# A two-layer decoder trunk: the index projection ordered by hand, PSUM banks swapped, three gate projections moved

## The chip, the cores and the metric

The kernel runs on one core of a Trainium2 chip. A core has five engines that work side by side and wait for one another through semaphores: TensorE (PE in the profile; its weight loads are PEld), VectorE (DVE), ScalarE (ACT), GpSimd (POOL) and SyncE (SP), which here only issues transfers. The metric is the device time of one execution, in microseconds. The time before is 760.7 us, the median of three runs (760.47 to 761.76).

## The reference, cut to what matters

`x` is 512 positions by 1024 channels, float32. Layer 0 is a gated mixer (a matrix memory and causal pooling); layer 1 is sparse attention. Layer 1 in short:

```python
xn = rmsnorm(x, g_norm)
q, ckv, qi, ki, wi, z = _split(xn @ w_in, ODD_SPLITS)   # 1024, 256, 4*64, 64, 4, 1024 columns
q = rmsnorm(q.reshape(hd), g_q)                         # 16 heads x 64
ckv = rmsnorm(ckv, g_kv)
k = rmsnorm((ckv @ w_uk).reshape(hd), g_k)
v = (ckv @ w_uv).reshape(hd)
# for each block of 128 queries
score = einsum('bqh,bqhs->bqs', wib, relu(einsum('bqhd,bsd->bqhs', qib, ki)))   # causal
_, idx = lax.top_k(score, 128)
logits = einsum('bqhd,bqkhd->bqhk', qb, k[idx]) * C_HEAD_DIM ** -0.5 + bias
out = einsum('bqhk,bqkhd->bqhd', softmax(logits), v[idx])
return x + (out * jax.nn.silu(z)) @ w_out
```

So three things come out of one input projection that matter below: the index part (`qi`, `ki`, `wi`, 324 columns), which decides which keys each query may see; the gates `z` (1024 columns, 64 for each of 16 heads); and the query and latent parts that feed the attention.

## The kernel before, in words

Activations lie with channels on the 128 partitions (`xT`, `xn_h`, `xn_l`: 8 blocks of 128 channels by 512 tokens). Every large product is made of three float32r matmuls: high part by high part, and the two mixed ones. So each weight tile is loaded by SP (`raw`), its high part cast on ACT (`wh`, L147), and its low part subtracted on DVE or POOL (`wl`, L148). A capital letter in an order list puts that subtraction on DVE, a small one on POOL. Three such tiles are in flight.

Layer 0 ends with its output projection. `next_x` (L605) adds a channel block to `xT` on DVE (L606), stores it, scales it into `xn_h` and `xn_l` (L241 on ACT, L242 on DVE), squares it (L250 on ACT) and adds the square to `ssum` on POOL (L251). `norm_factors` (L253) then sums `ssum` over the partitions on PE (L257), adds the epsilon on DVE, takes the power on POOL (L260, `r4`) and spreads the factors over the partitions with one more product (L265), copied on ACT to `r_bc`. `xn` of layer 1 is not yet normalised: the factors are applied where a projection's result leaves PSUM.

Layer 1 begins with the index projection: four token tiles `t` of 128, each of 8 channel blocks times 3 matmuls of 324 columns (L180 to L182). `ev_idx` (L637) scales the result on ACT into `qk_tok` (L640, L641), transposes it on PE (L645) and splits it into `qi` and `ki`. Then an order list, `ORDER` (L54), runs the steps: `i` scores of a query block, `C` the latent projection, `s` a quarter of a block's selection (rounds of MAX8, L725, and MATCH_REPLACE8, L726, on DVE), `q`, `k`, `v` projections of a group of four heads, `z` the gates of a group (two blocks of 24 matmuls of 512 columns, scaled on DVE, L803, SiLU on ACT, L804), `a` the attention of a group and a query block (exponential on ACT, L834, normalising on ACT, L836, transposes on PE, L844, product with v, L853 to L855, gate on DVE, L859), and `y` the split of finished results. The output projection of layer 1 follows.

What a list gives is a priority, not the last word. `TileContext(schedule_with_timeline_sim=True)` plans the order on each engine from estimated costs: where an instruction isn't ready in the plan, a later one goes ahead. Each engine then executes its queue strictly in that order.

PSUM has eight banks of 128x512 float32. `psum_pools` closes the pools and lays new ones from the first bank on. Layer 0 has `mm=4` in the first four banks and `bg=4` in the others. Layer 1 has `mm=3, qk=1, tr=2, po=1` (a `qk` tile takes two banks); `bg()` then means `tr`. A new tile waits for those who still use the bank.

Of the kernel before, what the change touches and what calls it, by code (L numbers as in the profile page):

```python
# [12 lines left out]
ALU = mybir.AluOpType  # L13
# [4 lines left out]
NT = 4  # L18
NK = 8
# [31 lines left out]
ORDER_A = ("z0 E0 k0 Q0 O0 W0 R0 Q1 k1 W1 R1 E1 v2 Y0 O1 Q2 k2 W2 k3 V3 z1 R2 q3 W3 R3 Y1")  # L51


ORDER = ("i1 i2 C i3 s10 q0 z0 k0 z2 v0 s11 v1 Z1 K1 Q1 s12 s13 s20 s21 s22 a00 Z3 s30 s23 s31 K2 s32 a01 a02 a10 s33 a12 a03 q2 V2 k3 a20 a23 a21 a13 a11 Q3 V3 a22 a33 a31 a32 y32 y31 y0 a30 y33 y30 y1 y2")  # L54


@with_exitstack
def trunk(ctx: ExitStack, tc: tile.TileContext, a: dict, out: bass.AP):
    nc = tc.nc
    V, A, G, T = nc.vector, nc.scalar, nc.gpsimd, nc.tensor  # L60
# [5 lines left out]
    ps = {}  # L66
    ps_pools = ExitStack()

    def psum_pools(**banks):
        ps_pools.close()  # L70
        ps.clear()
        for n, b in banks.items():
            ps[n] = ps_pools.enter_context(tc.tile_pool(name="ps_" + n, bufs=b, space=PSUM))

    ctx.callback(ps_pools.close)
    psum_pools(mm=4, bg=4)

    def bank(n):
        return ps[n].tile([128, 512], F32, name=n)

    def mm():
        return bank("mm")
    dr = ctx.enter_context(tc.tile_pool(name="dr", bufs=1, space=bass.MemoryType.DRAM))

    def bg():
        return bank("bg" if "bg" in ps else "tr")
# [3 lines left out]
    ident = cst[:, O_IDENT:O_IDENT + 128]  # L90
# [20 lines left out]
    def sub_f32r(dst, src, h):  # L111
        V.tensor_tensor(dst, src, h.bitcast(F32), op=ALU.subtract)  # L112

    def split(h, l, src):
        A.copy(h, src)  # L115
        sub_f32r(l, src, h)
# [9 lines left out]
    def run(order, **step):  # L126
        for w in order.split():
            low_engine[0] = V if w[0].isupper() else G
            step[w[0].lower()](*map(int, w[1:]))
# [4 lines left out]
    def wtile(shape, loads, queue=nc.sync):  # L134
        n = math.prod(shape)
        raw = wp.tile([128, 1024], F32, name="raw", bufs=3)
        wh = wp.tile([128, 1024], F32R, name="wh")
        wl = wp.tile([128, 1024], F32R, name="wl")

        def view(t):  # L140
            t = t[:, :n]
            if len(shape) == 2:
                t = t.rearrange("p (x y) -> p x y", x=shape[0])
            return t
        for sl, src in loads:
            queue.dma_start(view(raw)[:, sl[0], sl[1]], src)
        A.copy(wh[:, :n], raw[:, :n])  # L147
        low_engine[0].tensor_tensor(wl[:, :n], raw[:, :n], wh[:, :n].bitcast(F32), op=ALU.subtract)  # L148
        return view(wh), view(wl)
# [3 lines left out]
    def wrows(w, r0, nk, c0, n):  # L153
        return w[r0:r0 + 128 * nk, c0:c0 + n].rearrange("(k p) c -> p k c", p=128)

    def wcols(cols, kk, queue=nc.sync):
        loads, off = [], 0
        for w, c0, m in cols:
            loads.append(((ALL, slice(off, off + m)), wrows(w, 128 * kk[0], len(kk), c0, m)))
            off += m  # L160
        return wtile([len(kk), off], loads, queue)

    def dense_tok(act, ks, cols, evac, groups=(range(NT),), share=False):

        n = sum(x[2] for x in cols)
        step = min(1024 // n, len(ks))
        ws = {}

        def part(t, k0, ps):
            kk = ks[k0:k0 + step]
            if k0 not in ws:
                ws[k0] = wcols(cols, kk)
            wh, wl = ws[k0]
            for j, k in enumerate(kk):
                ah, al = act(k)
                ts = slice(128 * t, 128 * t + 128)
                first, last = (k0 + j == 0), (k0 + j == len(ks) - 1)
                T.matmul(ps, ah[:, ts], wh[:, j], start=first, stop=False)  # L180
                T.matmul(ps, ah[:, ts], wl[:, j], start=False, stop=False)  # L181
                T.matmul(ps, al[:, ts], wh[:, j], start=False, stop=last)  # L182

        for tts in groups:
            if share:
                two = mm().rearrange("p (u c) -> p u c", u=2)
                for u, t in enumerate(tts):
                    for k0 in range(0, len(ks), step):
                        part(t, k0, two[:, u])
                evac(tts[0], two)  # L190
                continue
            acc = {t: mm() for t in tts}
            for k0 in range(0, len(ks), step):
                for t in tts:
                    part(t, k0, acc[t][:, :n])
                    if k0 + step >= len(ks):
                        evac(t, acc[t])

    def dense_ch(act, w, c0, evac, r0=0):

        ps = mm()
        part_ch(act, wtile([NK, 128], [((ALL, ALL), wrows(w, r0, NK, c0, 128))]), range(NK), ps)
        evac(ps)
# [25 lines left out]
    xn_h = per.tile([128, NK, S], F32R, name="xn_h")  # L229
    xn_l = per.tile([128, NK, S], F32R, name="xn_l")  # L230
    xn = lambda k: (xn_h[:, k], xn_l[:, k])
    ones = nm.tile([128, 128], F32, name="ones")
    V.memset(ones, 1.0)
    ssum = nm.tile([128, S], F32, name="ssum")
# [9 lines left out]
    def squares(k):  # L244

        if k == 0:
            A.activation(ssum, xT[:, k], AF.Square, scale=1.0 / 32)
            return
        sq = nm.tile([128, S], F32, name="sq", bufs=2)
        A.activation(sq, xT[:, k], AF.Square, scale=1.0 / 32)  # L250
        G.tensor_tensor(ssum, ssum, sq, op=ALU.add)  # L251

    def norm_factors():  # L253

        p = bg()
        for t in range(NT):
            T.matmul(p[:, t:t + 1], ssum[:, 128 * t:128 * t + 128], ones[:, 0:1], start=True, stop=True)  # L257
        ss = sm.tile([128, NT], F32, name="n_ss")
        V.tensor_scalar(ss, p[:, 0:NT], EPS, None, op0=ALU.add)
        G.tensor_tensor(r4, ss, mhalf[:, :NT], op=ALU.pow)  # L260
        dg = nm.tile([128, NT, 128], F32, name="n_dg", tag="sq", bufs=2)
        V.tensor_tensor(dg, ident[:, None, :].to_broadcast([128, NT, 128]),
                        r4[:, :, None].to_broadcast([128, NT, 128]), op=ALU.mult)
        p = bg()
        T.matmul(p, ones, dg.rearrange("p t c -> p (t c)"), start=True, stop=True)  # L265
        A.copy(r_bc, p)


    warm = nm.tile([128, S], mybir.dt.bfloat16, name="warm")
# [9 lines left out]
    def arrive(k):  # L279
        nc.sync.dma_start(xT[:, k], xv[:, k])  # L280
        if k == 0:
            nc.sync.dma_start(e_g, a["e_norm"])
        scaled(y_h[:, k], y_l[:, k], k, e_g)
        squares(k)

    arrive(0)
    for k in range(NK):
        low_engine[0] = V if k % 2 == 0 else G
        wh, wl = wcols([(a["e_w_in"], 2048, 256), (a["e_w_in"], 5120, 264)], [k], nc.scalar if k < 2 else nc.sync)
        wh, wl = wh[:, 0], wl[:, 0]  # L290
# [9 lines left out]
        for t in range(NT):  # L300
            ts = slice(128 * t, 128 * t + 128)
# [35 lines left out]
    w_in, w_out = a["e_w_in"], a["e_w_out"]  # L337
# [267 lines left out]
    def next_x(c, ps):  # L605
        V.tensor_tensor(xT[:, c], ps, xT[:, c], op=ALU.add)  # L606
        nc.sync.dma_start(x_one[c], xT[:, c])
        scaled(xn_h[:, c], xn_l[:, c], c, o_g)
        squares(c)

    dense_ch4(y, w_out, 0, next_x, lambda c: mm())
    for c in range(4, NK):
        dense_ch(y, w_out, 128 * c, lambda ps: next_x(c, ps))
    norm_factors()
    V.tensor_scalar(r16, r4, 1.0 / 16, None, op0=ALU.mult)

    y_pool.close()

    w_in, w_out = a["o_w_in"], a["o_w_out"]
    w_uk, w_uv = a["o_w_uk"], a["o_w_uv"]  # L620
    psum_pools(mm=3, qk=1, tr=2, po=1)
    GR = ((0, 1), (2, 3))
    p2 = ctx.enter_context(tc.tile_pool(name="p2", bufs=1))
    zy = p2.tile([128, 8, S], F32, name="zy")
# [9 lines left out]
    ki_h, ki_l = (p2.tile([128, S], F32R, name=n, tag=n, bufs=3) for n in ("ak_h", "ak_l"))  # L634
    wi = p1.tile([128, NT, 4], F32, name="wi")

    def ev_idx(t, ps):  # L637
        qk = t1.tile([128, 6, 64], F32, name="qk_tok", tag="cb")
        r = r4[:, t:t + 1]
        A.activation(qk[:, 0:5], ps[:, 0:320].rearrange("p (h c) -> p h c", h=5), AF.Copy, scale=r)  # L640
        A.copy(qk[:, 5], qk[:, 4])  # L641
        A.activation(wi[:, t], ps[:, 320:324], AF.Copy, scale=r16[:, t:t + 1])
        p = bg()[:, 0:384].rearrange("p (c t) -> p c t", c=3)
        for c in range(3):
            T.transpose(p[:, c], qk[:, 2 * c:2 * c + 2], ident)  # L645
        ts = slice(128 * t, 128 * t + 128)
        split(qi_h[:, :, ts], qi_l[:, :, ts], p[:, 0:2])
        split(ki_h[:, ts], ki_l[:, ts], p[:, 2])
    low_engine[0] = G
    dense_tok(xn, range(NK), [(w_in, 1280, 324)], ev_idx, [(t,) for t in range(NT)])  # L650


    ckv_h = p1.tile([128, 2, S], F32R, name="ckv_h")
# [212 lines left out]
    step = dict(i=scores, c=ckv_proj, q=q_proj, k=k_proj, v=v_proj, z=z_proj, s=select, a=attend, y=y_split)  # L866
    run(ORDER, **step)

# [46 lines left out]
```

## Time and profile before

| what | before |
| --- | --- |
| median of three runs | 760.7 us |
| the profiled execution | 760.41 us |
| its span, first to last instruction | 758.6 us |
| mean granted TensorE clock | 0.997 |
| PE busy | 733.3 us (97%) |
| DVE busy | 458.2 us (60%) |
| ACT busy | 383.8 us (51%) |
| POOL busy | 304.2 us (40%) |

Times in the views count from the first instruction of the span. Layer 1 begins at about 464 us of them. A PE that is busy is not at its peak, since its matmuls overlap and their ends are modelled; an idle time in brackets is time in which the engine had nothing to execute, with what ended it. Busy times of one engine in a stretch are unions, so the stretch less the busy time is the engine's idle time. The chain that ended last is followed back from the last instruction: at each step to what released it, or else to the instruction before it on the same engine.

### The profile page before, as it was taken

The page shows a single profiled execution, that of the slowest core. Times are in us where ns is not written, and L with a number is a line of the kernel's source. Part 1 is how long each engine was busy: PE and PEld are TensorE (multiplying, and loading weights), DVE is VectorE, ACT ScalarE, POOL GpSimd, SP SyncE. Part 2 cuts the span into 40 slices and gives each one's busy share as a digit, 9 for nine tenths or more (in the row PEclk, how much of TensorE's full clock was granted, in tenths as well). Part 3 has the DMA queues.
Part 4 walks back from the last instruction along what each step waited for, and adds up shares of the span by engine and source line. Part 5 has one row for each costly group of instructions (what it writes and reads, how often), then busy time and mean ns, then how long its engine had stood idle before and what let it go on. Part 6 is the DMA issues. An engine that isn't in the chain of part 4 may idle for free.

```text
span 758.6 us, 11075 instructions
## 1 busy us (share of the span) xinstructions
PE 733.3 (97%) x4123; PEld 621.4 (82%) x4123; DVE 458.2 (60%) x944; ACT 383.8 (51%) x724; POOL 304.2 (40%) x254
## 2 busy tenths in 40 slices
PE   8989999999999999999999999999999998999987
PEld 6887888887888889888988888988898996777776
DVE  6686533434635866235514573399999986788531
ACT  6445333272535544344633453453565775998710
POOL 5455547723002011031363376246234752753321
PEclk9999999999999999999999999999999999999999
DMA  7623342345231323333322143513331220110061
GB/s 223 166 71 86 84 111 70 111 124 153 83 96 59 91 90 88 92 91 93 84 84 84 56 152 114 140 42 88 94 98 57 65 89 29 57 57 1 13 210 55
DMA packets 83989, 69.19 MB, mean 91 GB/s; under 512 B 3884, under 2 KB 71900, under 8 KB 83936
## 3 DMA queue, kind: packets, MB, share of 16 engines
q1 hardware_dynamic: 82144, 65.83, 30.2%
q10 hardware_dynamic: 1760, 2.66, 1.0%
q8 instruction: 32, 0.52, 0.3%
q14 instruction: 21, 0.17, 0.1%
q0 software_dynamic: 32, 0.01, 0.0%
HBM read 64.25 MB, written 4.23 MB: 90 GB/s over the span
## 4 chain that ended last, share of the span: by engine, by line
PE 79%; DVE 12%; ACT 5%; issue 2%; POOL 1%; DMA 1%; SPq 0%; DVEq 0%; POOLq 0%; ACTq 0%
PE mm L209 13%; PE mm L210 13%; PE mm L211 13%; PE mm L180 7%; PE mm L181 7%; PE mm L182 7%; DVE sel L726 1%; ACT lg L834 1%; DVE m L725 1%; DVE sel L718 1%; DVE pt_l L112 1%; PE qk L209 1%; ACT wh L147 1%; PE qk L211 1%; DVE wl L148 1%
## 5 line engine op out<-in xcount | busy, mean ns | idle before, releaser
L148 POOL TENSOR_TENSOR wl<-raw,wh 128x1024 fp32r<-128x1024 f32 (+4 forms) x65 | 148.5, 2285 | 265.0 <-ACT wh L147 220.8
L147 ACT CAST wh<-raw 128x1024 fp32r<-128x1024 f32 (+4 forms) x117 | 113.5, 972 | 175.5 <-PE mm L210 54.4
L209 PE MATMUL mm<-xn_h,wh 128*128 128x512 f32 x336 | 132.5, 396 | 4.4 <-DVE v_l L374 1.9
L210 PE MATMUL mm<-xn_l,wh 128*128 128x512 f32 x336 | 132.3, 394 | 0.0
L211 PE MATMUL mm<-xn_h,wl 128*128 128x512 f32 x336 | 131.9, 392 | 0.0
L182 PE MATMUL mm<-wh,xn_l 128*128 128x256 f32 (+2 forms) x384 | 123.6, 323 | 0.0
L181 PE MATMUL mm<-wl,xn_h 128*128 128x256 f32 (+2 forms) x384 | 123.5, 322 | 0.0
L180 PE MATMUL mm<-wh,xn_h 128*128 128x256 f32 (+2 forms) x384 | 120.8, 323 | 0.9 <-DVE xT L606 0.9
L148 DVE TENSOR_TENSOR wl<-raw,wh 128x1024 fp32r<-128x1024 f32 (+2 forms) x52 | 65.8, 1266 | 63.0 <-ACT wh L147 62.9
L180 PEld LDWEIGHTS mm<-wh,xn_h 128*128 128x128 f32 x384 | 72.0, 188 | 8.3 <-ACT wh L147 1.3
L209 PEld LDWEIGHTS mm<-xn_h,wh 128*128 128x128 f32 x336 | 63.1, 188 | 18.3 <-DVE v_l L374 2.0
L182 PEld LDWEIGHTS mm<-wh,xn_l 128*128 128x128 f32 x384 | 72.2, 188 | 6.4 <-issue 0.6
L181 PEld LDWEIGHTS mm<-wl,xn_h 128*128 128x128 f32 x384 | 72.2, 188 | 6.3 <-issue 0.5
L210 PEld LDWEIGHTS mm<-xn_l,wh 128*128 128x128 f32 x336 | 63.3, 188 | 14.1 <-issue 0.6
L211 PEld LDWEIGHTS mm<-xn_h,wl 128*128 128x128 f32 x336 | 63.2, 188 | 13.9
L211 PE MATMUL mm<-y_h,wl 128*128 128x512 f32 x128 | 50.2, 394 | 0.4 <-DVE wl L148 0.4
L210 PE MATMUL mm<-y_l,wh 128*128 128x512 f32 x128 | 50.3, 393 | 0.0
L209 PE MATMUL mm<-y_h,wh 128*128 128x512 f32 x128 | 48.8, 394 | 0.9 <-ACT y_h L115 0.9
L515 DVE SCALAR_TENSOR_TENSOR cv<-mm,s_conv,cv 128x511 f32<-128x511 f32 (+2 forms) x48 | 35.8, 746 | 16.2 <-ACT cv L513 15.3
L124 POOL TENSOR_TENSOR q_r<-q_ss,mhalf 128x8 f32<-128x8 f32 x16 | 27.2, 1701 | 40.5 <-DVE q_ss L121 32.7
L834 ACT ACTIVATE lg<-lg,st 128x128 f32<-128x128 f32 (+3 forms) x64 | 35.8, 561 | 9.4 <-DVE st L832 9.3
L836 ACT ACTIVATE lg<-lg,st 128x128 f32<-128x128 f32 (+3 forms) x64 | 34.0, 560 | 4.1 <-DVE st L835 3.9
(274 smaller groups left out, 1529.0 us busy)
## 6 DMA issues: line engine op xcount, KB each, us to landing
raw<-in_e_w_in_dram SPq DMA_DIRECT2D x52, 512.0 KB, 3.8
raw<-in_o_w_in_dram SPq DMA_DIRECT2D x18, 512.0 KB, 3.9
raw<-in_e_w_out_dram SPq DMA_DIRECT2D x16, 512.0 KB, 3.7
raw<-in_o_w_out_dram SPq DMA_DIRECT2D x8, 512.0 KB, 3.5
xT<-in_xT_dram SPq DMA_DIRECT2D x8, 256.0 KB, 3.7
x_one<-xT SPq DMA_DIRECT2D x8, 256.0 KB, 2.7
abias<-lines SPq DMA_DIRECT2D x4, 512.0 KB, 3.9
o_sb<-x_one SPq DMA_DIRECT2D x8, 256.0 KB, 4.0
```

The source lines that it names most:

```text
L124: G.tensor_tensor(dst, ss, mhalf[:, :n], op=ALU.pow)
L147: A.copy(wh[:, :n], raw[:, :n])
L148: low_engine[0].tensor_tensor(wl[:, :n], raw[:, :n], wh[:, :n].bitcast(F32), op=ALU.subtract)
L180: T.matmul(ps, ah[:, ts], wh[:, j], start=first, stop=False)
L181: T.matmul(ps, ah[:, ts], wl[:, j], start=False, stop=False)
L182: T.matmul(ps, al[:, ts], wh[:, j], start=False, stop=last)
L209: T.matmul(ps, wh[:, j], ah, start=(k == 0), stop=False)
L210: T.matmul(ps, wh[:, j], al, start=False, stop=False)
L211: T.matmul(ps, wl[:, j], ah, start=False, stop=(k == NK - 1))
L515: V.scalar_tensor_tensor(u[:, j:], ps[:, :S - j], w[:, 3 - j:4 - j], u[:, j:], op0=ALU.mult, op1=ALU.add)
L834: A.activation(lg[:, :n], lg[:, :n], AF.Exp, scale=-1.0, bias=st[:, 0:1], accum_out=st[:, 1:2])
L836: A.activation(lg[:, :n], lg[:, :n], AF.Copy, scale=st[:, 2:3])
```

## The change

Five edits, all in the order or the place of work; what is computed stays.

- Layer 0's PSUM pools are laid the other way: `bg` in the first four banks, `mm` in the last four.
- The last of the seven additions into `ssum` goes from POOL to DVE, in both layers.
- Layer 1's PSUM pools are opened before `norm_factors`, which therefore uses `tr` banks.
- The index projection is written out. The order on PE is fixed at four points with `tc.issue_after`, which orders instructions of one engine and adds no wait for a result: tile 1 comes behind the sums of `norm_factors`; tile 1's last two channel blocks behind tile 0's transposes; tiles 2 and 3, from their fourth block on, behind the transposes of tiles 1 and 2.
- In `ORDER`, `z2` goes from behind `k0` to behind `k3`, `Z3` from behind `a00` to behind `a11`, and `Z1` from behind `v1` to behind `s20`.

```diff
-ORDER = ("i1 i2 C i3 s10 q0 z0 k0 z2 v0 s11 v1 Z1 K1 Q1 s12 s13 s20 s21 s22 a00 Z3 s30 s23 s31 K2 s32 a01 a02 a10 s33 a12 a03 q2 V2 k3 a20 a23 a21 a13 a11 Q3 V3 a22 a33 a31 a32 y32 y31 y0 a30 y33 y30 y1 y2")
+ORDER = ("i1 i2 C i3 s10 q0 z0 k0 v0 s11 v1 K1 Q1 s12 s13 s20 Z1 s21 s22 a00 s30 s23 s31 K2 s32 a01 a02 a10 s33 a12 a03 q2 V2 k3 z2 a20 a23 a21 a13 a11 Z3 Q3 V3 a22 a33 a31 a32 y32 y31 y0 a30 y33 y30 y1 y2")
...
-    psum_pools(mm=4, bg=4)
+    psum_pools(bg=4, mm=4)
...
-        G.tensor_tensor(ssum, ssum, sq, op=ALU.add)
+        (V if k == NK - 1 else G).tensor_tensor(ssum, ssum, sq, op=ALU.add)
...
-    norm_factors()
+    psum_pools(mm=3, qk=1, tr=2, po=1)
+    sums = norm_factors()
...
+    def idx_part(t, k0):
+
+        kk = range(k0, min(k0 + 3, NK))
+        if k0 not in idx_w:
+            idx_w[k0] = wcols([(w_in, 1280, 324)], kk)
+        wh, wl = idx_w[k0]
+        ps, ts = idx_acc[t][:, :324], slice(128 * t, 128 * t + 128)
+        for j, k in enumerate(kk):
+            T.matmul(ps, xn_h[:, k, ts], wh[:, j], start=(k == 0), stop=False)
+            T.matmul(ps, xn_h[:, k, ts], wl[:, j], start=False, stop=False)
+            T.matmul(ps, xn_l[:, k, ts], wh[:, j], start=False, stop=(k == NK - 1))
...
-    dense_tok(xn, range(NK), [(w_in, 1280, 324)], ev_idx, [(t,) for t in range(NT)])
+    idx_w = {}
+    for t in range(NT):
+        idx_acc[t] = mm()
+        for k0 in (0, 3, 6):
+            behind = {(1, 0): sums, (1, 6): idx_tr.get(0), (2, 3): idx_tr.get(1), (3, 3): idx_tr.get(2)}.get((t, k0))
+            with tc.issue_after(behind.ins) if behind else ExitStack():
+                idx_part(t, k0)
+        idx_evac(t)
```

`idx_evac` is `ev_idx` under another name; it also keeps each tile's last transpose in `idx_tr`, and `norm_factors` returns its last sum.

## Rows read from the trace of the kernel before

**Rows 1.** The page of the whole span: busy time of each engine; DVE in 40 slices.

```profile
PE 733.3 (97%) x4123; PEld 621.4 (82%) x4123; DVE 458.2 (60%) x944; ACT 383.8 (51%) x724; POOL 304.2 (40%) x254
...
DVE  6686533434635866235514573399999986788531
```

**Rows 2.** Busy time by stretch, layer 1: us, PE, PEld, DVE, ACT, POOL (instructions), clock, DMA.

```profile
464.00:489.00 25.00, 24.53 (x180) 23.55 (x180) 6.09 (x11) 9.35 (x25) 7.36 (x6) 1.00 0.50 139
489.00:597.00 108.00, 106.16 (x719) 94.58 (x719) 104.87 (x262) 60.61 (x118) 50.14 (x44) 1.00 0.28 78
597.00:655.00 58.00, 54.38 (x430) 48.53 (x426) 44.17 (x132) 40.53 (x98) 27.91 (x37) 0.97 0.14 43
655.00:728.00 73.00, 66.72 (x445) 53.76 (x444) 54.28 (x183) 60.25 (x148) 36.15 (x46) 1.00 0.18 60
728.00:758.60 30.60, 25.31 (x108) 20.14 (x108) 6.15 (x10) 2.50 (x3) 4.80 (x2) 0.98 0.29 99
```

**Rows 3.** Timeline of PE, index chain: start, us, instruction, count [idle before, releaser].

```profile
464.47 0.39 PE L180 MATMUL mm<-wh,xn_h 128*128 128x324 f32 x1 [0.88 <-DVE xT L606]
...
470.02 0.95 PE L257 MATMUL bg<-ones,ssum 128*128 128x1 f32 x8
...
480.37 0.82 PE L645 MATMUL tr<-cst,qk_tok 128*128 128x128 f32 x6
...
486.80 0.39 PE L679 MATMUL qk<-ak_h,aq_h 64*128 64x256 f32 x1
```

**Rows 4.** Timelines of DVE, POOL and ACT over the same stretch.

```profile
465.12 1.22 DVE L242 SCALAR_TENSOR_TENSOR xn_l<-xT,o_g,xn_h 128x512 fp32r<-128x512 f32 x1 [0.79 <-ACT xn_h L241]
465.75 1.74 POOL L251 TENSOR_TENSOR ssum<-ssum,sq 128x512 f32<-128x512 f32 x1
471.25 1.02 POOL L260 TENSOR_TENSOR r<-n_ss,mhalf 128x4 f32<-128x4 f32 x1 [3.76 <-DVE n_ss L259]
473.17 0.24 ACT L641 COPY qk_tok<-qk_tok 128x64 f32<-128x64 f32 x1
489.38 0.48 DVE L718 SCALAR_TENSOR_TENSOR sel<-relu,wi,sel 128x256 f32<-128x256 f32 x1
```

**Rows 5.** The tile sel: min, median, max ns; first and last start.

```profile
L725 DVE MAX8 m<-sel x48: 410/551/695, 492.4 to 596.7; 128x8 f32<-128x256 f32 x16, 128x8 f32<-128x384 f32 x16, 128x8 f32<-128x512 f32 x16
```

**Rows 6.** Timeline of PE after the selection: instructions before which PE sat idle.

```profile
627.44 0.65 PE L679 MATMUL qk<-ak_h,aq_h 64*128 64x512 f32 x1 [1.73 <-DVE st L832]
...
698.33 0.39 PE L853 MATMUL po<-pt_h,av_h 128*128 128x256 f32 x1 [0.84 <-DVE st L832]
```

**Rows 7.** Timelines of DVE and ACT around Z3.

```profile
572.50 1.23 DVE L148 TENSOR_TENSOR wl<-raw,wh 128x1024 fp32r<-128x1024 f32 x1 [0.47 <-ACT wh L147]
578.74 0.67 DVE L803 TENSOR_TENSOR zy<-mm,r_bc 128x512 f32<-128x512 f32 x1
578.49 1.05 ACT L147 CAST wh<-raw 128x1024 fp32r<-128x1024 f32 x1 [3.47 <-PE mm L210]
580.14 1.28 ACT L804 ACT_TABLE_LOAD   x1
581.44 0.64 ACT L804 ACTIVATE zy<-zy 128x512 f32<-128x512 f32 x1
587.59 1.28 ACT L834 ACT_TABLE_LOAD   x1
```

**Rows 8.** Chain that ended last, 597 to 655, then 655 to 688: shares of the stretch.

```profile
by line: ACT lg L834 8.0%; DVE pt_l L112 7.6%; issue 6.3%; DVE lg L832 5.8%; DVE zy L859 5.0%; ACT lg L836 4.8%; PE po L855 4.8%; DVE q_ss L757 4.4%; DVE wl L148 4.1%; ACT wh L147 4.1%; PE tr L844 4.1%; ACT q_sq L755 3.7%; PE qk L682 3.4%; 
by line: ACT lg L834 17.3%; ACT lg L836 12.8%; DMA abias<-lines 11.2%; DVE pt_l L112 9.1%; ACT pt_h L115 7.3%; issue 5.9%; DVE zy L859 4.9%; POOL cb L829 4.4%; DVE lg L832 4.3%; ACT wh L147 2.9%; DVE aq_l L770 2.3%; POOL sel L829 2.3%; POOL
```

**Rows 9.** Timelines of DVE and POOL at the start of layer 0.

```profile
7.45 0.70 DVE L148 TENSOR_TENSOR wl<-raw,wh 128x520 fp32r<-128x520 f32 x1 [0.28 <-ACT wh L147]
12.37 1.80 DVE L148 TENSOR_TENSOR wl<-raw,wh 128x520 fp32r<-128x520 f32 x1
16.99 5.14 POOL L251 TENSOR_TENSOR ssum<-ssum,sq 128x512 f32<-128x512 f32 x3
```

More of the change, by code (lines that the diff above doesn't have):

```diff
@@ L256, in norm_factors @@
         for t in range(NT):
-            T.matmul(p[:, t:t + 1], ssum[:, 128 * t:128 * t + 128], ones[:, 0:1], start=True, stop=True)
+            sums = T.matmul(p[:, t:t + 1], ssum[:, 128 * t:128 * t + 128], ones[:, 0:1], start=True, stop=True)
         ss = sm.tile([128, NT], F32, name="n_ss")
@@ L266, in norm_factors @@
         A.copy(r_bc, p)
+        return sums
     warm = nm.tile([128, S], mybir.dt.bfloat16, name="warm")
@@ L620, in trunk @@
     w_uk, w_uv = a["o_w_uk"], a["o_w_uv"]
-    psum_pools(mm=3, qk=1, tr=2, po=1)
     GR = ((0, 1), (2, 3))
@@ L635, in trunk, with idx_evac @@
     wi = p1.tile([128, NT, 4], F32, name="wi")
-    def ev_idx(t, ps):
+    idx_acc, idx_tr = {}, {}
+    def idx_part(t, k0):
[8 more added lines that the diff above has]
+            T.matmul(ps, xn_l[:, k, ts], wh[:, j], start=False, stop=(k == NK - 1))
+    def idx_evac(t):
+        ps = idx_acc[t]
         qk = t1.tile([128, 6, 64], F32, name="qk_tok", tag="cb")
@@ L644, in ev_idx @@
         for c in range(3):
-            T.transpose(p[:, c], qk[:, 2 * c:2 * c + 2], ident)
+            idx_tr[t] = T.transpose(p[:, c], qk[:, 2 * c:2 * c + 2], ident)
         ts = slice(128 * t, 128 * t + 128)
```

## The prediction, made before the change was built

> **What bounds the kernel now.** I read four views: the page for the engines' shares, the busy time by stretch, the chain that ended last, and the timelines around the edit. The page says TensorE first: PE is busy 97% of the span, DVE 60% [rows 1]. DVE's digits show one block of nines in the second half, so I cut layer 1 into stretches [rows 2]. From 464 to 489 PE works (24.53 of 25.00 us) while DVE idles (6.09): the index projection and its norm. From 489 to 597 both are full: PE 106.16 and DVE 104.87 of 108. DVE's load there is the top-k selection; its 48 MAX8 start at 492.4 and end at 596.7 [rows 5]. From 597 to 728 most of the attention runs and no engine is full: PE idles 3.62 and 6.28 us, DVE 13.8 and 18.7, ACT 17.5 and 12.8 [rows 2]. The chain passes there from ACT to DVE to PE in small steps [rows 8]. After 728 the output projection alone remains. It is 108 matmuls and the stores, 30.6 us that the change doesn't touch.
>
> So the end moves with the end of the attention, and there are two ways to move it: a DVE that begins selecting sooner, and PE work that fills its waits after 597. PE sets the cap. Between 463.6 and 728 it idles 0.88 us ahead of the first index matmul [rows 3] and 1.84, 3.62 and 6.28 us in the three later stretches [rows 2]. No ordering of this work gains more than these 12.6 us, short of matmuls issued more densely.
>
> **The change part by part.** *Banks.* The first index matmul waits 0.88 us for DVE's last addition on xT [rows 3], although its first operands, channel block 0, were ready long before: its bank is one from which the output projection is still read. With bg in front, the new mm banks are the old bg ones, which were idle by then. The wait goes: -0.9. What is late next is block 7, whose low part ends at 465.12 + 1.22 = 466.3 [rows 4]. Token tile 0 reaches it after 21 matmuls; 37 in a row take 470.02 - 464.47 = 5.55 us [rows 3], 0.15 each, so at 463.6 + 3.2 = 466.8. It is covered.
>
> *Last square sum on DVE.* On POOL it ends at 465.75 + 1.74 = 467.5 [rows 4]. On DVE it follows the low part from 466.3 and costs what a 128x512 operation costs there, 0.67 [rows 7]: 467.0. The edit also acts in layer 0. There DVE can't begin before POOL's preceding sums end at 16.99 + 5.14 = 22.1, and the same DVE operation has taken 0.70 and 1.80 us at different moments [rows 9]. Weight splits queue behind it, and PE waits for those. Bounds: a gain of 0.3 to a loss of 1.1. I take 0, since PE's place for these sums there comes later anyhow.
>
> *Index chain.* Now the sums' matmuls stand in PE's order at 470.02, 2.5 us after they could run. The first transposes stand at 480.37, though qk_tok was written by 473.4 [rows 3, 4]. In the new order everything of tile 1 queues behind the sums, and parts of tiles 1 to 3 behind the transposes of the tile before. Worked out: tile 0 (24 matmuls, 3.6 us) ends at 467.2; sums 0.95, so 468.15; DVE's addition and POOL's power (1.02 [rows 4]) give r4 at about 469.4 and qk_tok at 470.2. PE meanwhile does 18 matmuls (2.7 us) to 470.85 and transposes tile 0 without a wait. Six and nine matmuls later come those of tile 1 (473.5), and after 24 more those of tile 2 (477.5). PE runs out of index work at about 480.2. If any link is late, all of PE queues behind it: a late sum, a late qk_tok, or the copy of r_bc that frees the transposes' second buffer. Four such points at 0 to 0.4 us bound this at 0 to 1.5; I take 0.3, because the cover worked out for each link is longer than the link. Banks and stalls together: -0.6.
>
> Block 1's scores need tiles 0 and 1 alone. They could run at 475.4, but rank behind the index matmuls in the program, so I put them at 480.2 instead of 486.8 [rows 3], a lead of 6.6 us. The bounds are 2.8 (the sums' own lead) and 11.4. DVE can take it: its first score operation is at 489.38 [rows 4], and it idles most of the 18 us before. With DVE full until the last MAX8, the selection then ends near 590.
>
> *z later.* z2 and Z3, heads 8 to 15, move behind the projections before a20 and Q3; Z1 moves by five entries only. Each step is 48 matmuls of 512 columns, and I spread these at 0.23 us (108 such matmuls in 25.31 us [rows 2]): 22 us of PE work leave the full stretch. So do 4 x 0.67 us on DVE and two of its weight splits of 1.23 [rows 7], 5.1 us in all. Their successors (K1, Q1, K2, q2, V2, k3) come sooner by as much PE time, which lets the attention start when the selection does. These need more of DVE per PE microsecond, so PE may wait more before 590: bounds -1.8 (the 1.84 of idle goes) to +4 (an estimate: a fifth of 22 us uncovered). I take 0, as the lead and the 5.1 us relieve DVE. The four weight transfers and z2's splits on POOL move with the steps. POOL is busy 50.14 of 108 and then 27.91 of 58 us, and the DMA share is 0.14 where they land [rows 2]: nothing.
>
> After 590, 96 matmuls that wait for no attention stand in PE's queue. PE's 3.62 us of idle from 597 to 655 are single waits on DVE, up to 1.73 us [rows 6], beside which such matmuls fit. I take all of it: -3.6. Of the 6.28 us after 655 (0.84, say [rows 6]) filler reaches only the first half, and the earlier start moves some of the rest away; I take half: -3.1.
>
> The price falls on ACT: four casts of 1.05 and four SiLUs of 0.64 [rows 7], 6.8 us, come among the exponentials, plus table loads. Z3 cost two loads of 1.28 [rows 7]; two separate z steps amid exponentials cost four, so +2.6. The bounds are 0, if both share one pair, and +7.7, if each SiLU has its own. Of these 9.4 us the share counts that ACT has in the chain there. The rows name 8.0 + 4.8 + 4.1 + 3.7 = 21% [rows 8]: +2.0.
>
> The trace shows the load to be 1.28 us with SiLU 0.02 us behind it [rows 7]. The Trainium skill speaks against this change here: "ScalarE: Activation LUTs", sections What ACT_TABLE_LOAD costs and Table sets, says to batch functions by set, since a switch costs 1283 ns and a drain of 1380 more. With its price for two more loads the sum would be 0.6 later; no idle time in these rows shows that drain, so the sum goes by the row.
>
> **Sum.** -0.6 - 3.6 - 3.1 + 2.0 = -5.3. The profiled execution took 760.4 us, 1.8 of it outside its span of 758.6: 755.1. The median of the runs is 760.7 and they spread from 760.5 to 761.8, so the basis is good to about 1 us. About 0.2% (1.5 us) is what can be told from no change.
>
> **The rivals.** *All of the lead is used* (0.22). With the selection ending at 590 and projections ahead, PE's idle after 597 goes whole, and ACT takes its extra work in its own 17.5 us of idle: -0.9 - 9.9 = 749.6; 745 to 751.5. For it: ACT idles most just where z lands. Against it: the small steps in the chain, which filler doesn't shorten.
>
> *The lead ends in another wait* (0.12). The planner keeps the order after the index chain much as it was, or the attention is held by the last projections and by the load of abias, which alone is 11.2% of the chain from 655 to 688 [rows 8]. Then only the head gains: 759.8, within 1.5 either way.
>
> *ACT becomes the bound* (0.20), the slower side. If each of the four SiLUs falls between exponentials, ACT gets 6.8 + 7.7 = 14.5 us. If z also slips past 655, ACT's share of the chain is 17.3 + 12.8 + 7.3 + 2.9 = 40% [rows 8], and the fill comes where PE waits for ACT anyhow. Then 760.4 - 0.6 + 5.8 = 765.6; own range 761 to 769. It decides once over half of the 14.5 us is on the path, as that eats the 7.3 us of gains. Against it: ACT is busy 40.53 of 58 us until 655.
>
> **How the numbers follow.** The forecast has 0.46, with its own range 751.5 to 758.5. Faster by over 0.2%: 0.46 + 0.22 and a little of the third case, 0.70. Same: 0.10. Slower: 0.20. The range takes in the second case down to 747 and the slower one up to 764; about 0.18 is left out.
>
> **What would show it.** Right: no gap ahead of the first index matmul; the sums about 467.5; block 1's scores near 480 and the first MAX8 near 486; the last MAX8 near 590; z's matmuls at 590 to 640 with less PE idle there; the granted clock, 0.97 from 597 to 655 now [rows 2], nearer 1.00; output projection alone from about 723. Wrong: the selection ends at 597 as before, or PE waits for DVE before 590; more than four table loads around z2 and Z3 with ACT full and PE idle beside it; or PE idle of several tenths behind the sums or transposes.

## The result, and the profile after

The changed kernel takes 769.98 us (median of four runs, 769.28 to 770.78); before, in the same comparison, 761.23. The ratio is 1.0116, with a 95% interval of 1.0098 to 1.0134: slower by some 9 us, where 755.1 was forecast and 764 was the end of the range. The profiled execution took 769.28 us, its span is 767.5.

First the page of after: busy time by engine, and DVE in 40 slices (before: [rows 1]).

```profile
PE 734.2 (96%) x4123; PEld 621.9 (81%) x4123; DVE 466.0 (61%) x946; ACT 390.6 (51%) x728; POOL 302.2 (39%) x252
...
DVE  6696434344727765147224573699999964878631
```

PE's work is the same to a microsecond (733.3 before), the span is 8.9 us longer. So PE waits. The busy time by stretch, to be held against [rows 2] (columns as there), says where:

```profile
464.00:489.00 25.00, 24.35 (x175) 22.45 (x174) 9.65 (x15) 10.28 (x26) 5.36 (x5) 1.00 0.40 114
489.00:597.00 108.00, 99.08 (x732) 90.45 (x732) 105.52 (x266) 60.15 (x122) 52.06 (x50) 0.98 0.23 68
597.00:655.00 58.00, 55.69 (x371) 48.25 (x370) 40.23 (x114) 39.83 (x79) 21.32 (x30) 1.00 0.22 68
655.00:728.00 73.00, 64.82 (x445) 53.02 (x444) 55.56 (x182) 63.02 (x158) 36.23 (x47) 0.98 0.09 30
728.00:767.50 39.50, 33.73 (x155) 27.09 (x153) 10.75 (x22) 6.43 (x10) 9.63 (x4) 0.98 0.39 133
```

From 489 to 597 PE idles 108 - 99.08 = 8.92 us, where it idled 1.84. That alone is 7.1 of the 8.9 us. DVE is as full there as before (105.52 against 104.87). The later stretches are shifted, so I cut the last 130 us before the last product with v ends (727.6 before, 736.5 after) into two parts. First before, then after, same columns:

```profile
597.60:655.10 57.50, 53.85 (x424) 48.18 (x422) 43.67 (x131) 40.03 (x97) 28.01 (x38) 0.97 0.14 43
655.10:727.60 72.50, 66.65 (x444) 53.76 (x444) 53.79 (x181) 60.15 (x148) 36.05 (x45) 1.00 0.17 58
```

```profile
606.50:664.00 57.50, 54.90 (x369) 46.59 (x369) 38.34 (x105) 42.81 (x83) 22.03 (x26) 1.00 0.15 51
664.00:736.50 72.50, 65.66 (x438) 54.24 (x438) 52.26 (x175) 57.95 (x143) 34.44 (x44) 0.98 0.14 48
```

PE idles 3.65 + 5.85 = 9.50 us there before and 2.60 + 6.84 = 9.44 after. The matmuls moved to this part filled nothing on balance. From the last product with v to the end it is 31.0 us in both.

Now the head. The timeline of PE (start, duration, instruction), to be held against [rows 3]:

```profile
463.02 0.31 PE L648 MATMUL mm<-wh,xn_h 128*128 128x324 f32 x1
...
466.69 1.02 PE L257 MATMUL tr<-ones,ssum 128*128 128x1 f32 x8
...
472.53 0.49 PE L661 MATMUL tr<-cst,qk_tok 128*128 128x128 f32 x3
...
480.73 0.38 PE L704 MATMUL qk<-ak_h,aq_h 64*128 64x256 f32 x1
```

No gap stands ahead of the first index matmul, the sums come 3.3 us sooner, the first transposes 7.8, block 1's scores 6.1. But the tile sel (minimum, median, maximum in ns; first and last start), to be held against [rows 5], shows that the selection made nothing of it. The second line is the score operation on DVE; its counterpart before ran from 477 to 2607 ns:

```profile
L750 DVE MAX8 m<-sel x48: 414/552/692, 491.5 to 606.5; 128x8 f32<-128x256 f32 x16, 128x8 f32<-128x384 f32 x16, 128x8 f32<-128x512 f32 x16
...
L743 DVE SCALAR_TENSOR_TENSOR sel<-relu,wi,sel x12: 481/738/2771, 486.0 to 513.3; 128x256 f32<-128x256 f32 x4, 128x384 f32<-128x384 f32 x4, 128x512 f32<-128x512 f32 x4
```

The first MAX8 starts 0.9 us sooner, not 6; the last 9.8 us later. What PE waited for from 463 to 601 (us in total, times, longest; the four longest):

```profile
PE tr L695 <- DVE c_n L691: 3.0, 1, 3.0
PE mm L180 <- DVE av_l L112: 2.6, 1, 2.6
PE qk L704 <- DVE st L857: 1.8, 1, 1.8
PE tr L792 <- DVE q_n L788: 1.5, 2, 1.2
```

These are waits for the latent norm (`c_n`), the split of v, the first attention and the query norm, all on DVE, all queued there among selection rounds. Before, in that stretch, only q_n was waited for (1.1 us), and the evacuations of a gate (0.8) and of `xT` (0.9). To this the clock adds: the granted clock of two stretches of after, the first of them right behind the wait for c_n:

```profile
506.80:510.20 3.40, 3.36 (x15) 3.07 (x17) 3.33 (x10) 0.59 (x1) 0.00 (x0) 0.50 0.00 0
670.60:674.00 3.40, 3.40 (x16) 3.40 (x17) 1.36 (x7) 2.14 (x6) 1.46 (x2) 0.50 0.34 132
```

0.50 is the lower of the two levels, 1.2 GHz. Ahead of the second stand two shorter waits of PE, of 1.03 us to 669.2 and of 0.79 us to 670.5. Between the first index matmul and the last product with v there was one such stretch before and there are two in after: 1.7 us more.

The books between these two points: before 727.6 - 464.5 = 263.1 us, of it 11.3 idle and 1.7 lost to the clock; after 736.5 - 463.0 = 273.5, of it 20.1 and 3.4. What remains is 250.1 and 250.0 us. The end has moved by -1.5 (the earlier start) + 8.8 (idle) + 1.7 (clock) = 9.0; the spans say 8.9.

### The profile page after: what moved, and what is told of

It reads as the page before. It is cut to its first block, busy times and chain, and to the rows that moved or that the text cites. A ratio compares the mean times of both kernels' runs of the same rounds, so it can differ in the third digit from the quotient of the medians.

```text
span 767.5 us, 11082 instructions
## 1 busy us (share of the span) xinstructions
PE 734.2 (96%) x4123; PEld 621.9 (81%) x4123; DVE 466.0 (61%) x946; ACT 390.6 (51%) x728; POOL 302.2 (39%) x252
## 4 chain that ended last, share of the span: by engine, by line
PE 75%; DVE 15%; ACT 4%; issue 3%; POOL 1%; DMA 1%; SPq 0%; DVEq 0%; ACTq 0%; POOLq 0%
PE mm L209 13%; PE mm L211 13%; PE mm L210 13%; PE mm L180 6%; PE mm L181 6%; PE mm L182 6%; DVE sel L751 2%; DVE sel L743 2%; DVE m L750 2%; PE tr L869 1%; DVE wl L148 1%; PE po L878 1%; PE po L880 1%; PE qk L209 1%; DVE sq L314 1%
## 5 line engine op out<-in xcount | busy, mean ns | idle before, releaser
L181 PE MATMUL mm<-wl,xn_h 128*128 128x256 f32 (+1 forms) x352 | 113.7, 323 | 0.4 <-DVE wl L148 0.4
L182 PE MATMUL mm<-wh,xn_l 128*128 128x256 f32 (+1 forms) x352 | 113.5, 323 | 0.0
L180 PE MATMUL mm<-wh,xn_h 128*128 128x256 f32 (+1 forms) x352 | 111.5, 325 | 0.3 <-ACT wh L147 0.3
L210 PEld LDWEIGHTS mm<-xn_l,wh 128*128 128x128 f32 x336 | 63.2, 188 | 13.2 <-DVE pt_l L112 0.4
L180 PEld LDWEIGHTS mm<-wh,xn_h 128*128 128x128 f32 x352 | 66.4, 189 | 7.0 <-issue 0.6
L181 PEld LDWEIGHTS mm<-wl,xn_h 128*128 128x128 f32 x352 | 66.5, 189 | 6.8 <-DVE wl L148 0.6
L182 PEld LDWEIGHTS mm<-wh,xn_l 128*128 128x128 f32 x352 | 66.6, 189 | 5.8
L859 ACT ACTIVATE lg<-lg,st 128x128 f32<-128x128 f32 (+3 forms) x64 | 35.7, 559 | 11.0 <-DVE st L857 10.6
```

What stands on the lines that cost most here:

```text
L210: T.matmul(ps, wh[:, j], al, start=False, stop=False)
L859: A.activation(lg[:, :n], lg[:, :n], AF.Exp, scale=-1.0, bias=st[:, 0:1], accum_out=st[:, 1:2])
```

## Experiments

My theory after the result: z2's matmuls were the cover for PE while DVE selects, and without them every link of the projections that passes through DVE shows (A). The rival B: the index chain and the banks cost the time. Later theories came with the runs; the quotes name them by letter. All results in one table: the difference is to the median of before in the same comparison (761.8 to 762.5 there); "idle" is PE's from the first index matmul to the last product with v, the length of that stretch less PE's busy time in it, and "clock" the mean granted clock of that stretch. Both are of the one profiled execution. After was timed in a comparison of its own, in which before took 761.2, so differences between its row and the others are good to about 1 us: by the medians themselves e4, e8 and e12 give back 6.3, 9.2 and 5.8 us, by the differences 7.4, 10.1 and 6.3.

| kernel | median us | difference | ratio (95%) | idle us | clock |
| --- | --- | --- | --- | --- | --- |
| before | | 0 | 1 | 11.3 | 0.994 |
| after | 769.98 | +8.7 | 1.0116 (1.0098 to 1.0134) | 20.1 | 0.988 |
| e1_old_order | 767.24 | +4.8 | 1.0065 (1.0050 to 1.0081) | 15.4 | 0.987 |
| e2_order_only | 768.02 | +5.6 | 1.0072 (1.0049 to 1.0095) | 16.6 | 0.987 |
| e3_banks_only | 773.08 | +10.6 | 1.0139 (1.0120 to 1.0158) | 13.7 | 0.991 |
| e4_z2_back | 763.72 | +1.3 | 1.0025 (1.0014 to 1.0037) | 14.3 | 0.994 |
| e5_add_only | 763.00 | +0.8 | 1.0018 (1.0007 to 1.0029) | 14.2 | 0.994 |
| e6_banks_pools | 767.03 | +4.8 | 1.0071 (1.0048 to 1.0095) | 15.6 | 0.987 |
| e7_z2_back_C_first | 762.36 | +0.2 | 1.0004 (0.9993 to 1.0015) | 13.8 | 0.994 |
| e8_splits_on_dve | 760.77 | -1.4 | 0.9983 (0.9968 to 0.9998) | 13.2 | 0.987 |
| e9_before_dve_splits | 760.25 | -1.6 | 0.9975 (0.9962 to 0.9988) | 9.4 | 0.994 |
| e10_z2_back_dve_splits | 758.30 | -3.5 | 0.9959 (0.9945 to 0.9973) | 10.8 | 1.000 |
| e11_old_order_dve_splits | 760.04 | -1.8 | 0.9983 (0.9971 to 0.9996) | 11.6 | 0.994 |
| e12_selection_behind_cn | 764.23 | +2.4 | 1.0026 (1.0013 to 1.0039) | 15.0 | 0.987 |

### The parts alone

e1 is after with the order list of before; e2 is before with the new list; e3 is before with the banks swapped and nothing else; e4 is after with z2 back in its place.

```diff
 e1, against after:   ORDER = the list of before
 e2, against before:  ORDER = the list of after
 e3, against before:
-    psum_pools(mm=4, bg=4)
+    psum_pools(bg=4, mm=4)
 e4, against after:
-i3 s10 q0 z0 k0 v0 ... k3 z2 a20
+i3 s10 q0 z0 k0 z2 v0 ... k3 a20
```

> The changed kernel with the order list of before: index chain, banks and the addition on DVE stay changed, the z steps stand where they stood. Theory A (the z steps covered PE's waits during the selection, and the loss is that cover): the time goes back to that of before, 759 to 762 us, PE idle from 489 to 597 near 2 us. Theory B (the order fixed on PE for the index chain puts latent matmuls ahead of the last index tile and delays the chain's consumers): it stays near 768 to 771.

> The kernel of before with the new order list alone. Theory A: the whole loss, 768 to 771 us, with PE idle from 489 to 600 near 9 us and the last MAX8 some 8 to 10 us later than before. Theory B: near 761 us.

> The kernel of before with the two PSUM pools of layer 0 laid the other way, and nothing else. Both theories: the wait of 0.88 us ahead of the first index matmul goes; the time is 0 to 1 us under that of before, unless the planner orders something else differently.

> The changed kernel with z2 alone back behind k0; Z1 and Z3 stay late. Theory A: about half of the loss comes back, 763 to 767 us, as z2 is the z step that stands in the first part of the selection, where PE idles in the changed kernel (3.0 us at 504, 1.2 at 520, 2.6 near 533). Theory B: no change from 770.

e2's 768.0 us lies where theory A had it, but against before in its comparison the list alone costs 5.6 us, not the whole 8.7, and the last MAX8 starts at 617.0, 20 us later than before instead of 8 to 10. And e1, with the old list, also costs 4.8, which A excludes. Neither theory is enough; each half costs by itself and the two don't add (4.8 + 5.6 is more than 8.7). e4 gives back 7.4 of the 8.7 us for one list entry, more than the half that was expected: A holds for z2, in this kernel. There the wait for c_n is still 3.0 us long, but those for av_l and st are gone.

e3 failed for a reason of its own. What PE waited for in it from 463 to 490:

```profile
PE bg L257 <- POOL ssum L251: 3.9, 1, 3.9
PE bg L265 <- DVE r L615: 2.2, 1, 2.2
PE mm L180 <- ACT r_bc L266: 0.7, 1, 0.7
```

With bg in front, the sums and `r_bc` use banks that layer 1's mm tiles need, and the index projection can't begin before `r_bc` is copied: its first matmul stood at 475.9 (the idle of e3 in the table begins there, and leaves these waits out). The pools that after opens before `norm_factors` therefore belong to the swap.

### The smaller edits

e5 is before with the last addition on DVE; e6 is before with the swap and the pools opened early; e7 is e4 with `C` ahead of the scores.

```diff
 e5, against before:
-        G.tensor_tensor(ssum, ssum, sq, op=ALU.add)
+        (V if k == NK - 1 else G).tensor_tensor(ssum, ssum, sq, op=ALU.add)
 e6, against before:
-    psum_pools(mm=4, bg=4)
+    psum_pools(bg=4, mm=4)
...
+    psum_pools(mm=3, qk=1, tr=2, po=1)
     norm_factors()
...
-    psum_pools(mm=3, qk=1, tr=2, po=1)
 e7, against e4:
-ORDER = ("i1 i2 C i3 s10
+ORDER = ("C i1 i2 i3 s10
```

> The kernel of before with the last addition into ssum on DVE, in both layers, and nothing else. Theory C (any small edit lets the planner lay out another order, and the orders of layer 1 differ by several us for that alone): 2 us or more away from before, in either direction, with other waits in layer 1. Theory D (the loss of the index part comes from what its edits do, not from a new layout): within 1 us of before, and the sums' matmuls not earlier than before, as their place on PE is unchanged.

> The kernel of before with the PSUM pools swapped and those of layer 1 opened ahead of the norm's sums, as in the changed kernel; the index projection, the addition and the order list as before. In the run with the swap alone the first index tile had to wait until r_bc was copied out of its bank (6.8 us of PE idle). With the pools opened first that wait is expected gone, and so is the 0.88 us of before: 0 to 1.5 us under before (theory D). Theory C: several us away from it.

> The changed kernel with z2 back behind k0 (763.7 us) and the latent projection C ahead of the scores i1 and i2 in the order list. In the changed kernel PE waits 3.0 us at 504 for c_n, which DVE executes behind rounds of the selection, and the clock then falls for 3.4 us. Theory E (those 3.0 us and the clock are the index part's loss): the wait goes and 3 to 5 us with it, 758.5 to 761. Rival (the wait is only moved, as DVE is full either way): 762.5 to 765.

e5 costs 0.8 us by the medians (0.5 to 2.2 by the interval), about what theory D allowed. e6, where theory D failed, is the most telling of these: the gap of 0.88 us is gone, the index matmuls start at 464.0, the last MAX8 ends at 590.1 (before 597.3), all as the prediction wanted it, and yet the last product with v ends 6.0 us later than before. First e6, then e7: what PE waited for from 463 to 601 (the two longest).

```profile
PE tr L767 <- DVE q_n L763: 4.0, 2, 3.0
PE tr L670 <- DVE c_n L666: 0.5, 1, 0.5
```

```profile
PE tr L792 <- DVE q_n L788: 3.7, 2, 2.6
PE tr L695 <- DVE c_n L691: 0.6, 1, 0.6
```

In e6 the selection ran ahead of the query norm in DVE's queue, and PE waited for that: the norm's factor was written at 516.4, and DVE got to q_n at 518.4. In e7 the wait for c_n shrank from 3.0 us (e4) to 0.6, and those for q_n grew from 2.2 to 3.7, so the time fell by 1.4 us only, where theory E had 3 to 5. A selection that ends sooner is no gain; where it stands ahead of the projections' norms it is a loss.

### The weight splits

In after three of the first score operations took over 2 us. POOL and DVE of after side by side, by start:

```profile
486.70 2.40 POOL L148 TENSOR_TENSOR wl<-raw,wh 128x1024 fp32r<-128x1024 f32 x1 [13.25 <-ACT wh L147]
487.04 2.35 DVE L743 SCALAR_TENSOR_TENSOR sel<-relu,wi,sel 128x256 f32<-128x256 f32 x1 [0.60 <-ACT relu L742]
489.84 0.48 DVE L743 SCALAR_TENSOR_TENSOR sel<-relu,wi,sel 128x256 f32<-128x256 f32 x1 [0.45 <-ACT relu L742]
...
495.25 2.39 POOL L148 TENSOR_TENSOR wl<-raw,wh 128x1024 fp32r<-128x1024 f32 x1 [1.05 <-ACT wh L147]
495.28 2.77 DVE L743 SCALAR_TENSOR_TENSOR sel<-relu,wi,sel 128x384 f32<-128x384 f32 x1
...
501.11 2.40 POOL L148 TENSOR_TENSOR wl<-raw,wh 128x1024 fp32r<-128x1024 f32 x1
501.65 2.27 DVE L743 SCALAR_TENSOR_TENSOR sel<-relu,wi,sel 128x384 f32<-128x384 f32 x1
...
506.22 0.87 DVE L691 SCALAR_TENSOR_TENSOR c_n<-mm,c_r,b_o_g_kv 128x256 f32<-128x256 f32 x2
```

Each long operation starts within a split on POOL and ends 0.29 to 0.41 us behind its end; alone it takes 0.48 (256 columns) or 0.60 (384). The three cost 1.87 + 2.17 + 1.67 = 5.7 us of DVE, ahead of c_n. The fourth split of q0 and z0, at 516.92, meets a DVE operation too, behind c_n: the small scaling of `q_ss` at 517.50 takes 1.87 us, where the one before it took 0.15. The same splits also stand in POOL's own queue, which POOL executes in order: between the two POOL steps of c_n's factor (`c_r`, 500.45 and 503.46) lies the split of 501.11. e8 takes the four splits of q0 and z0 off POOL; e9 does that to before, e10 to e4, e11 to e1:

```diff
-s10 q0 z0 k0
+s10 Q0 Z0 k0
```

> The changed kernel with the weight splits of q0 and z0 on DVE (1.23 us each) in place of POOL (2.4 us each). Theory F (DVE's score operations, 0.48 to 0.6 us alone, take 2.3 to 2.8 where POOL splits weights beside them, three times, and that is where the head start of the index chain is lost): no score operation over 1 us, the PE wait for c_n under 1.5 us, time down by 2 to 5 us from 770. Rival (DVE is full, so the four splits cost it as much as they free): within 1.5 us of 770.

> The kernel before with only the weight splits of q0 and z0 on DVE instead of POOL. In the run where after had this edit alone, PE's idle time fell from 20.1 to 13.2 us. Theory F: a DVE operation of the scores stretches from 0.5 to 1.3-2.6 us beside a POOL split; in before three of them do, some 4 us, but there PE had z2's matmuls to do meanwhile and idled only 1.84 us from 489 to 597, so the edit has at most that to give: 759 to 763 us, ratio 0.996 to 1.002. Rival G (the relief is worth as much in any order): 752 to 756 us. Rival H (any other plan than before's costs several us by itself): 765 to 769 us.

> After with z2 back behind k0 and the splits of q0 and z0 on DVE. With z2 back alone it took 763.7 us with 14.3 us of PE idle. Theory F: both edits cover the same waits of PE (those for c_n, q_n and av_l between 500 and 537), so together they give little more than one: 759 to 762 us. Rival G (each gives its own gain, 6.3 and 9.2 us): 754 to 756 us, which would beat both kernels.

> After with the order list of before, and in it the splits of q0 and z0 on DVE: banks, addition and index chain are those of after, no z moves. With the order list of before alone it took 767.2 us, 15.4 us of PE idle, a half-clock window at 507-514. Theory F: the scores of blocks 1 and 2 lose their stretched operations, the wait for the latent norm goes and the half clock with it: 760 to 763 us. If the edit only helps where z is moved: 766 to 768 us. If the index chain's earlier start is then used by the selection: under 758 us.

e8 gives back more than the whole loss, and more than the 2 to 5 us that theory F had: from +8.7 to -1.4. On DVE a split takes 1.23 us and the score operations their 0.48 to 0.74, and c_n comes 6.6 us sooner. DVE in e8, then what PE waited for there from 463 to 601 (the first two lines):

```profile
494.15 0.62 DVE L743 SCALAR_TENSOR_TENSOR sel<-relu,wi,sel 128x384 f32<-128x384 f32 x1
...
499.61 0.87 DVE L691 SCALAR_TENSOR_TENSOR c_n<-mm,c_r,b_o_g_kv 128x256 f32<-128x256 f32 x2
```

```profile
PE mm L180 <- DVE av_l L112: 2.1, 1, 2.1
PE mm L209 <- DVE q_n L788: 1.1, 1, 1.1
```

The same edit gives before only 1.6 us (e9): there z2 stood as cover, and PE's idle had little to lose. It gives e1 6.6 us (e11), so what the index chain cost in e1 came from these splits too. In e10 it gives 4.8 us, not the 10 of e8: the two edits cover some of the same waits, as theory F had it, but less than I had reckoned, since 758.3 us lies below the 759 to 762 of F and above the 754 to 756 of G. It is 0.4% (0.27 to 0.55) faster than before and the fastest of these kernels. Busy time by stretch, to the last product with v, first e11, then e10:

```profile
489.00:597.00 108.00, 108.00 (x739) 96.56 (x738) 104.39 (x263) 60.87 (x115) 41.70 (x41) 1.00 0.30 84
597.00:655.00 58.00, 52.77 (x412) 46.95 (x410) 44.76 (x129) 39.58 (x95) 28.43 (x37) 0.97 0.13 42
655.00:727.90 72.90, 67.13 (x447) 53.85 (x445) 53.79 (x181) 60.48 (x149) 36.45 (x46) 1.00 0.18 59
```

```profile
489.00:597.00 108.00, 106.64 (x772) 96.74 (x771) 105.20 (x271) 62.18 (x122) 45.99 (x47) 1.00 0.28 77
597.00:655.00 58.00, 54.45 (x381) 46.28 (x380) 44.03 (x128) 43.93 (x94) 26.72 (x33) 1.00 0.19 60
655.00:725.70 70.70, 65.41 (x440) 52.72 (x438) 51.93 (x175) 58.39 (x145) 34.18 (x45) 1.00 0.16 50
```

Put side by side: with the splits on POOL the new list costs 5.6 us (e2), the new head (banks, pools, addition and index chain) 4.8 (e1) and both 8.7; with the splits on DVE, against e9, the new head costs nothing (e11, 760.04 against 760.25) and both cost 0.2 to 0.5 us (e8). So the loss goes with these splits on POOL, and without it the whole change is worth nothing rather than the 5.3 us forecast. The list alone with the splits on DVE was not run.

e11 has the head that I had predicted for PE: index matmuls at 463.6, PE not idle at all from 489 to 597 (its selection still runs from 491.1 to 596.7, not from 486 to 590). And it gains nothing over e9, which has none of it (760.04 and 760.25): PE then idles 5.23 us from 597 to 655, where before idled 3.62. What was saved ahead of the attention is waited for in it. e10 differs from e11 only in that Z1 and Z3 stand later. PE's idle after 597 is 3.55 + 5.29 = 8.8 us in it instead of 5.23 + 5.77 = 11.0. That is the fill that I had forecast, 2.2 us of it, at the price of 1.36 us of idle before 597. The half-clock stretch of e11 (0.97 from 597 to 655) is missing in e10, which is 1.7 us more in these two executions; it isn't in every one, since the mean granted clock of e11's ten executions ran from 0.993 to 0.999. The medians differ by 1.7.

### Order or collision

Moving the splits also changes DVE's order: in after 8 rounds of the selection stand ahead of the second c_n, in e8 5. e12 changes that order in after and leaves the splits on POOL:

```diff
+    cn_last = [None]
...
-            V.scalar_tensor_tensor(cn[:, u], ps[:, u], r[:, u:u + 1], gkv, op0=ALU.mult, op1=ALU.mult)
+            cn_last[0] = V.scalar_tensor_tensor(cn[:, u], ps[:, u], r[:, u:u + 1], gkv, op0=ALU.mult, op1=ALU.mult)
...
-        for _ in range(4):
+        with tc.issue_after(cn_last[0].ins) if (i, part) == (1, 1) else ExitStack():
+            for _ in range(4):
```

> After with one more order: rounds 5 to 8 of block 1's selection stand behind the second latent norm c_n on DVE. All weight splits of q0 and z0 stay on POOL. In after the second c_n starts at 506.2, behind 8 rounds; with the splits on DVE it started at 499.6, behind 5. Four rounds of 0.98 us less should bring it to about 502.5 here, by either theory, and PE's wait of 2.97 us for it should go. Theory F (beside a POOL split the score operations of blocks 1 to 3 stretch, 5.7 us in three of them, and all that follows on DVE is late by that): the later waits of PE, for q_n and for av_l's split, stay or grow; 766 to 770 us. Rival O (the loss is in the order of the DVE queue, which changed with the move of the splits): as with the splits on DVE, 759 to 763 us.

It fell between the two: +2.4, 6.3 of after's 8.7 us given back, where e8 gave 10.1. DVE in e12, then what PE waited for from 463 to 601:

```profile
495.71 2.77 DVE L745 SCALAR_TENSOR_TENSOR sel<-relu,wi,sel 128x384 f32<-128x384 f32 x1
...
503.49 0.88 DVE L693 SCALAR_TENSOR_TENSOR c_n<-mm,c_r,b_o_g_kv 128x256 f32<-128x256 f32 x2 [1.84 <-POOL c_r L691]
```

```profile
PE tr L795 <- DVE q_n L791: 2.5, 1, 2.5
PE mm L180 <- DVE av_l L112: 2.0, 1, 2.0
PE mm L209 <- DVE q_n L791: 1.1, 1, 1.1
```

The wait for c_n is gone without a split being moved: by this edit the place of the rounds in DVE's queue is the larger part. What the splits still cost is seen in three places. Two of the long score operations remain (2.34 and 2.77 us, 4.0 more than alone). c_n now waits 1.84 us for POOL, where its factor stands behind a split that runs from 500.86 to 503.3. And PE's next wait, 2.5 us for q_n, which e8 doesn't have, has the fourth split ahead of it. POOL and DVE of e12 side by side, by start:

```profile
514.53 2.39 POOL L148 TENSOR_TENSOR wl<-raw,wh 128x1024 fp32r<-128x1024 f32 x1
515.12 1.84 DVE L121 TENSOR_SCALAR q_ss<-q_ss 128x8 f32<-128x8 f32 x1
516.89 0.20 POOL L789 TENSOR_TENSOR q_r<-q_r,r 128x8 f32<-128x8 f32 x1
518.71 0.67 DVE L791 TENSOR_TENSOR q_n<-mm,q_r 128x512 f32<-128x512 f32 x1
```

The split holds back the second step of q_n's factor on POOL (`q_r`) and, beside it, DVE's small `q_ss`; the selection operations that follow `q_ss` then stand ahead of q_n. So 3.8 us lie between e12 and e8, but they can't be shared out among the blocked DVE operations, the splits' place in POOL's queue and the order on DVE: e8 takes the first two away at once, and each of these kernels was planned anew from the change on. No run keeps the splits on POOL and out of the factors' way.

## Why the prediction was wrong, point by point

*Where the gains lie.* "The end moves with the end of the attention": right, 31.0 us from the last product with v to the end in both. PE "sets the cap": right, 250 us of work lie in layer 1 before and after. Of the "two ways to move it" the first was wrong: "a DVE that begins selecting sooner" moved nothing in these runs. e6 ends the selection 7.2 us sooner than before and takes 4.8 longer; e8 ends it at 612.0, 14.7 later, and takes 1.4 less.

*Banks.* "The wait goes: -0.9": right, the wait is gone. The first index matmul moved from 464.5 to 463.0, but not all of these 1.5 us are the banks': in e2 and e9, whose layer 0 is that of before, it stands at 465.6 and 466.5, so single executions scatter by about 2 us there. That the pools must be opened ahead of `norm_factors` for it I hadn't seen; alone, the swap costs 10.6 us (e3).

*Last square sum.* Predicted to end at 467.0, measured 465.86 + 0.68 = 466.5. Alone it costs the whole kernel 0.8 us by the medians (e5), within the bounds of -0.3 to 1.1, though the interval (0.5 to 2.2) reaches beyond.

*Index chain.* Sums "468.15" at their end, measured 467.7; scores of block 1 "at 480.2", measured 480.73; no idle at the four points. The step that failed is the next one, "DVE can take it". The lead of 6.1 us at the scores was 0.9 at the first MAX8. ACT executes in order, and its first relu stood at 485.25 behind a weight cast at 483.73, which had waited for index matmuls to free its tile (1.19 us); then came the score operation that took 2.35 us beside POOL. The prediction had looked at DVE's idle time alone, not at the queue of ACT ahead of it, nor at POOL beside it.

*z later.* "I take 0, as the lead and the 5.1 us relieve DVE", with +4 as the upper bound. This is the step that cost the most: measured +7.1 us of idle from 489 to 597, of which the list alone makes 5.3 (e2). The bound took a fifth of 22 us as uncovered, an estimate with no row behind it. The right question was which links PE's remaining work passes through: c_n, q_n and av_l each go through DVE's queue, where rounds of the selection stand ahead of them (eight ahead of the second c_n). z2's matmuls need nothing from that queue until their result is evacuated, so they could run meanwhile. e4 shows what they were worth here: 7.4 us. With the four splits off POOL the same list costs 0.4 to 0.7 us (e8 against e11), so most of what z2 covered was, as it seems, what these splits held up; the prediction had weighed POOL by its busy share alone.

*Fill after the selection.* "I take all of it: -3.6" and "I take half: -3.1": measured -1.0 and +1.0 in the two parts of the last 130 us, together -0.1. PE's waits there are steps within one block's attention (the gate `zy` 3.0 us, `pt_l` 1.6 us in after), and a matmul placed ahead of them only moves the wait. Between e11 and e10, 2.2 us of such a gain is seen.

*The price on ACT.* "Two more loads": four more, nine against five from 464 on. But the rival that built on it (765.6, the nearest to the truth in its number) isn't what happened: e8 has eleven table loads from 464 on and is 9 to 10 us faster than after, and in after PE's waits of over 1.5 us are for DVE.

*What would have shown it.* The prediction's own sign against itself came: "PE waits for DVE before 590".

## What to carry to other kernels

Before work is taken out of a stretch in which two engines are full, list what PE will wait for there once it is gone: each link that passes through the other full engine's queue stands behind whatever that engine has ready, and a long product that needs nothing of it is cover, not ballast. Look for what runs on DVE and POOL at the same moment: the nine changed kernels with these four weight splits on POOL took 0.2 to 10.6 us longer than before, the four with them on DVE 1.4 to 3.5 us less. An earlier start was worth nothing by itself here; follow it through every queue to the next engine that is full, and to the end.

## What the runs showed of the hardware

Beside a POOL subtraction of two 128x1024 tiles in SBUF (2.40 us), a DVE operation with two such inputs is recorded as busy for 2.27 to 2.77 us instead of 0.48 to 0.60. These rows look like waiting, not like slower work: wherever in the split the operation began, it ends 0.29 us (256 columns) or 0.41 us (384 columns) behind POOL's end, and in before, at 512.20, 0.55 us (512 columns). The Trainium skill ("SBUF — State Buffer", section SBUF: two separate sides) describes it so: the read and write ports that DVE and GpSimd share are given to one of them for a whole instruction, and the other is blocked, among them a DVE instruction with two SBUF inputs against a GpSimd instruction that reads SBUF. The trace agrees: with POOL first by 0.03 us at 495.25, DVE's operation ends 0.41 us after the split. The small `q_ss` operation, which has one input, was held up too (1.87 us instead of 0.15, at 517.50, to within 0.04 us of the split's end), while a MAX8 that began at 501.31, inside a split, took its usual 0.43. So DVE's busy time in a full stretch can be waiting: of the 105.52 us of after from 489 to 597, at least 2.17 + 1.67 + 1.72 = 5.6 are.

The granted clock of TensorE fell to 0.50 (1.2 GHz) for 3.4 us behind PE's wait of 2.97 us in after, in e12 at 519.8, behind the one of 2.48 us, and in before at 627.6, behind the one of 1.73 us [rows 6]. Not every such wait brings this: behind the 2.58 us for av_l in after, which end at 535.4, the clock stays at 1.00 until 540. Each such stretch costs 1.7 us more, so the wait of 2.97 us cost nearly 5.
